# Copies of the relative bias's lines: one write per query row, or a read back to all partitions and a write from there

## The chip, the cores and the metric

One core of a Trainium2 chip runs one program: two transformer blocks over 256 tokens of width 1024 in float32. The metric is the device time of one execution in microseconds (us). In what follows TensorE is called PE as in the profile, VectorE DVE, ScalarE ACT, GpSimd POOL, and SP is the engine that issues the loads of the weights. POOL issues the few transfers that this change is about.

## What is computed

The first block has two layers, each a mixer and an MLP of 4096 hidden columns with a squared ReLU. The second block has a linear recurrence and a causal attention side by side, and a gated MLP. The attention adds a bias to each score which depends on the head and on the distance between query and key alone. Cut to what matters here (with 256 tokens there is one block of keys, so each query sees all keys up to itself):

```python
def sq_relu_mlp(x, w_up, w_down):
    h = jax.nn.relu(x @ w_up)
    return (h * h) @ w_down
...
table_h = rel_table.astype(f32).T
lo = jnp.einsum('bhqd,bhsd->bhqs', qc, ko).astype(f32) * scale
dist_o = tpos[:, None] - (cur * BLK + jnp.arange(BLK))[None, :]
lo = jnp.where(dist_o >= 0, lo + table_h[:, t5_bucket(dist_o)], -jnp.inf)
...
p = jax.nn.softmax(logits, axis=-1)
```

## The kernel before

**Tiling.** A token tile is 128 tokens (P = 128), there are two (TT). Every product with a weight runs as three float32r passes over a split of both sides into a high and a low part: `wh`, `wl` for weights and `xh`, `xl` (or `yh`, `yl` for an MLP's hidden columns) for activations.

**Weights.** They come in units of 256 rows x 512 columns (512 KB). For each unit SP issues a load into a buffer `raw` (line 231, five buffers), ACT casts it to `wh` (line 241, eight buffers) and DVE subtracts to get `wl` (line 242, eight buffers). A load is issued when the unit five before has been split and its `raw` is free; a cast goes on when PE has used the unit eight before. SP issues the loads in the order in which PE uses the units.

**Order on PE.** A small planner (`Line`) runs tasks that are generators: each yields how long after its last product its next operands are there, and of the tasks that can go on, the one of lowest rank does. What comes out is a fixed order of instructions on every engine; the order on DVE, ACT and POOL is made from it by a list scheduler at build time.

**The first block's MLPs.** Both (`mlp0` and `mlp1`) are the same program over eight blocks of 512 hidden columns: `up(b)` takes four units of `w_up`, and `down(b)` takes four units of `w_down`. In the trace the products of an `up` write `mm` (128x256) and those of a `down` write `acc` (128x512). After each `up` ACT applies the ReLU (line 629) and DVE squares it (line 630, tile `hid`).

**The relative bias.** While `mlp1` runs, a task `bias_line` (rank 2) builds `rline`: 8 partitions, one per head, each with a line of LN = 384 floats, which is the negative bias of each distance. It needs one small product (32 buckets x 256 distances) and a copy to SBUF (line 1134). Then POOL issues two transfers, one for four heads each (line 1137). Their destination is `line_d` in DRAM, of which every head has 128 rows that all hold the same line:

```python
line_d = dram.tile([NH, P, LN], F32, name="line_d")
...
nc.gpsimd.dma_start(line_d[hs], rline[hs, None, :].to_broadcast([4, P, LN]))
```

Each is thus 512 rows of 1,536 bytes (768 KB), all read from four partitions of SBUF.

After `mlp1`, in the second block, the task `rel_bias` reads `line_d` back with POOL into the tiles `rel` (line 1317, two transfers of 512 KB): query q's partition reads its row one element earlier than query q-1's, which gives the matrix of distances. DVE uses `rel` in the attention (line 1397).

Of the kernel before, what the change touches and what calls it, by code (L numbers as in the profile page):

```python
# [8 lines left out]
F32 = mybir.dt.float32  # L9
# [6 lines left out]
P = 128  # L16
# [7 lines left out]
# rows of the table of per-partition vectors  # L24
V_PSCALE, V_MQ, V_MK, V_SQ, V_SK, V_Q2, V_K2, V_HG, V_GAMMA, V_N = 0, 6, 8, 10, 11, 12, 13, 14, 15, 31
# and of the gains that go into the weights
# [3 lines left out]
def t5_starts():  # L30
    """First distance of each T5 bucket, and one past the last."""
    bucket = []
    for n in range(S):
        if n < 16:
            bucket.append(n)
        else:
            bucket.append(min(31, 16 + int(math.log(n / 16) / math.log(128 / 16) * 16)))
    return [bucket.index(b) for b in range(32)] + [1 << 20]
# [3 lines left out]
def kernel(  # L42
# [17 lines left out]
    class Stage:  # L60
        """The tiles of one stage; the next stage's take over their bytes."""
# [14 lines left out]
    class Event:  # L76
        """The time from which something is there, once that is known."""
# [6 lines left out]
    class Line:  # L84
        """Orders the tensor engine's work. A task is a generator that yields how long (us) after its last
        product its next one's operands are there, or events to wait for; of the tasks that can go on, the
        one with the lowest rank does."""
# [40 lines left out]
    class Slots:  # L128
        """Lets n tasks at a time hold the buffers of some work."""
# [50 lines left out]
    # -------------------------------------------------------- first loads  # L180
# [3 lines left out]
    # gains that go into the weights, and other small parameters, by feature  # L184
# [11 lines left out]
    # the activation tables are loaded while the first loads are under way  # L196
# [4 lines left out]
    def bcast(dst, vec, eng):  # L201
        """A vector in DRAM to every partition."""
        return eng.dma_start(
            dst, bass.AP(tensor=vec.tensor, offset=vec.offset, ap=[[0, P]] + [list(e) for e in vec.ap]))

    def gain(i):
        """Eight columns of gains, for the k-tiles."""
        return gcols[:, i:i + KT]

    # ------------------------------------------------------------- weights  # L210
    # All products run in float32r passes over exact splits a = hi + lo of both sides:
    # hi hi + hi lo + lo hi. Chunks of weights are loaded and split in the order of their use.
# [4 lines left out]
    def planned(key, segs, nk=KT, row0=0, g=None):  # L217
        """g: first column in gcols of the gains of the weights' rows."""
# [4 lines left out]
    def load_units(segs, nk, row0, g, apart=0):  # L223
        for k0 in range(0, nk, KU):
# [10 lines left out]
            # the split comes after other work that is ready: weights are loaded well ahead  # L235
# [19 lines left out]
    def W(key, ahead=KT):  # L255
        """The split k-tiles of a chunk; the next ones in the order of use are started."""
# [55 lines left out]
    def lin(acc, xt, w, start=True, stop=True):  # L312
        """acc[token, column] (+)= x w, with x as its transposed (hi, lo) k-tiles."""
# [9 lines left out]
    def lin_T(acc, xt, w, c0):  # L323
        """acc[column c0.., token] = (x w)^T."""
# [10 lines left out]
    # ------------------------------------------------------------ constants  # L335
# [4 lines left out]
    # ------------------------------------------------------------- helpers  # L340

    def power(dst, src):
        """src ** -0.5"""
        G.tensor_tensor(dst, src, mhalf[:, :src.shape[-1]], ALU.pow)  # L344

    def xset(name="x"):
        """hi and lo k-tiles of a transposed activation, [feature, k, token]."""
# [7 lines left out]
    def split_T(src, xs, tt, k0, n, by=None):  # L355
        """Columns of src (up to 4 tiles of 128, token-major) to k-tiles k0.. of xs, times by by feature."""
# [5 lines left out]
    def split(pt, xs, tt, k0, n, by=None):  # L362
        """A bank of n tiles to k-tiles k0.. of xs."""
# [15 lines left out]
    class Norm:  # L379
        """Mean square of the rows of a [P, D] tile, gathered by column halves."""  # L380
# [16 lines left out]
        def into(self, xs, tt, g, done):  # L397
            """Normed by the row and g, split and transposed to token tile tt of xs."""
# [20 lines left out]
    def head_rstd(src, nh, hd, sq, name="hs"):  # L419
        """(mean square + eps) ** -0.5 per head of src [P, nh, hd]; sq is scratch."""  # L420
# [7 lines left out]
    def head_norm(src, nh, hd, y):  # L428
        """src [P, nh, hd] over its root mean square per head (no gain) into y."""
# [7 lines left out]
    def exp_T(blocks):  # L437
        """Up to four [P, 128] blocks transposed, side by side."""
# [14 lines left out]
    def residual(tt, c, acc, last=True, lat=1.5, by=None):  # L453
        """h += acc (times by)."""
# [15 lines left out]
    def residual_r(tt, c, acc, last=True):  # L470
        """The one of the first MLP."""
# [4 lines left out]
    def residual_2(tt, c, acc, last=True):  # L476
        """The one of the second MLP."""
# [4 lines left out]
    def residual_ms(tt, c, acc, last=True):  # L482
        """The one before a squared ReLU; that gets h as it is, and its result the reciprocal mean squares."""
# [7 lines left out]
    def add_norms(*sets):  # L491
        """Tasks that write the normed h into sets, a list of (set, gain); the events of each set by token tile."""
# [11 lines left out]
    def turned(xs, src, tt, g, done):  # L504
        """src times the gains g by feature, if any, split and transposed to token tile tt of xs."""
# [5 lines left out]
    def add_turned(xs, g=None):  # L511
        """Tasks that write h to xs, and their events."""
# [19 lines left out]
    def mixer_out(key, xs, cuts, there):  # L532
        """Tasks of h += x w, the rows of w cut into groups; there[token tile][group] are the groups' events."""
# [13 lines left out]
    # ------------------------------------------------------------- the MLPs  # L547

    def mlp(key, xs, there, nb, ku, hidden, finish, ends=1):
        """h += hidden(x up) down in nb blocks of ku * 128 hidden columns; finish(tt, c, acc, last) takes the sums.  # L550
        The last block's part of the last ones can come by itself, in pieces."""
# [13 lines left out]
        def up_one(b, tt):  # L565
            """One token tile: through [token, hidden] and transposes."""
# [78 lines left out]
    # ----------------------------------------------- layer 0: first norms  # L645

    # In the mixers the norms' gains are in the weights, and the root mean squares are put on the products.
# [30 lines left out]
    # the pool mixer's input [feature, k-tile, token], and the queries for the memory  # L678
# [3 lines left out]
    # the pool mixer's windows by feature: k-tile, partitions, group of the window  # L682
# [3 lines left out]
    # window over count for the first tokens  # L686
# [13 lines left out]
    def raw_T():  # L700
        """For a transposed input as it is, in two halves of its k-tiles."""
# [20 lines left out]
    with tc.manual_schedule(engines={ET.DVE, ET.Activation, ET.Pool, ET.PE}):  # L722
        # the first products go on as inputs and weights come in
        x_raw, m_raw = raw_T(), raw_T()
        # products of ones let the tensor engine's clock come up before the weights are there
# [15 lines left out]
        def columns_T(ps, xs, w, k, c0):  # L741
            """More of ps[column, token] from the k-tiles w, which begin at k."""
# [34 lines left out]
        # the rows' root mean squares along the free axis, in every partition  # L777
# [46 lines left out]
    # ----------------------------------------------------- memory attention  # L824
# [3 lines left out]
    def add_mem_kv(l, rank, lat, accs=None):  # L828
        """Keys [feature, head pair, key] and values [key, tile, feature] of layer l, their events and the task;
        accs holds the products if they are under way, lat is the time of the keys' norm."""  # L830
# [13 lines left out]
    def keys_T(acc, r, kT, tt, done, lat):  # L844
        """Four normed heads of 64 in acc's first half to [feature, head pair, key]."""
# [10 lines left out]
    def mem_attention(l, q, xs, tt, q_there, done):  # L856
        """The result for queries q goes to k-tiles 6, 7 of xs."""
# [5 lines left out]
        # the scores get the root mean squares of their queries' heads in the exponential  # L863
# [7 lines left out]
        # the two halves of the array work side by side, into different banks  # L871
# [32 lines left out]
    # -------------------------------------------------- layer 0: pool mixer  # L904
# [669 lines left out]
```

## Time and profile before

| | |
|---|---|
| median of 3 runs | 1080.47 us (1078.93 to 1081.23) |
| the profiled execution, first to last instruction | 1079.3 us |
| PE busy | 1054.1 us (98%) |
| DVE, ACT, POOL busy | 643.0, 562.7, 122.8 us |
| HBM read, written | 181.00 MB, 2.62 MB |
| transfers issued by SP | 180.43 MB |
| transfers issued by POOL | 3.23 MB |

The profile gives the span from the first to the last instruction of one execution, and no other time of that execution. The span lies 1.2 us under the median of the runs and inside their range, so a sum made against the span is carried to the median by adding that difference. A queue's share in the table of DMA queues is the time that its packets took, over 16 DMA engines times the stretch: a share of 50% can be eight engines that are always at work or sixteen that are half the time.

### The profile page before, as it was taken

What the parts mean: (1) busy time and instruction counts of PE and PEld (TensorE: products, weight loads), DVE (VectorE), ACT (ScalarE), POOL (GpSimd) and SP (SyncE); (2) the same over time, 40 slices, a digit from 0 to 9 for tenths busy, and PEclk for the clock granted to TensorE, in tenths of its full rate; (3) what the DMA queues carried; (4) which work ended last, traced back from release to release, by engine and by line L of the source; (5) the groups of instructions that cost most, each with busy time, mean ns of one, the idle gap of its engine ahead of it and who ended that gap; (6) DMA issues with size and microseconds to landing.
All of it is one profiled execution on the core that took longest, in us unless ns stands there. A gap on an engine that the chain in (4) does not pass through costs nothing.

```text
span 1079.3 us, 18396 instructions
## 1 busy us (share of the span) xinstructions
PE 1054.1 (98%) x7352; PEld 927.5 (86%) x7352; DVE 643.0 (60%) x987; ACT 562.7 (52%) x901; POOL 122.8 (11%) x154
## 2 busy tenths in 40 slices
PE   8999999999999996999999998999999999999998
PEld 8768899988876785888988996888999988999997
DVE  5886654554687750755557559766645576454452
ACT  6766544544688640645456443757744466344341
POOL 0524000000152000000001007740000000000000
PEclk9999999999999998899999999999999999999999
DMA  9754465465461456765647552543455556564741
GB/s 317 255 174 157 159 201 187 157 195 195 156 195 41 134 139 116 235 202 177 209 137 232 199 193 81 158 136 113 143 192 182 174 177 213 157 209 150 225 139 40
DMA packets 108551, 184.84 MB, mean 171 GB/s; under 512 B 7769, under 2 KB 32601, under 8 KB 108465
## 3 DMA queue, kind: packets, MB, share of 16 engines
q1 hardware_dynamic: 106560, 180.43, 51.8%
q0 software_dynamic: 1904, 3.23, 2.0%
q8 instruction: 57, 0.93, 0.4%
q14 instruction: 30, 0.24, 0.1%
HBM read 181.00 MB, written 2.62 MB: 170 GB/s over the span
## 4 chain that ended last, share of the span: by engine, by line
PE 91%; DMA 4%; POOL 2%; issue 1%; DVE 1%; ACT 0%; SPq 0%; POOLq 0%; ACTq 0%
PE acc L152 56%; PE mm L152 32%; DMA raw<-in_w_down_dram 3%; PE mm L159 3%; POOL fK L1263 1%; DMA raw<-in_w_in_dram 1%; POOL win L916 0%; DVE wl L242 0%; POOL hs L344 0%; ACT wh L241 0%; POOL hn L431 0%; POOL st L415 0%; POOL win L915 0%; DVE wl L247 0%; POOL st L344 0%
## 5 line engine op out<-in xcount | busy, mean ns | idle before, releaser
L242 DVE TENSOR_TENSOR wl<-raw,wh 128x1024 fp32r<-128x1024 f32 (+1 forms) x315 | 380.6, 1231 | 207.5 <-ACT wh L241 205.1
L241 ACT CAST wh<-raw 128x1024 fp32r<-128x1024 f32 (+1 forms) x315 | 322.0, 1046 | 207.9 <-PE acc L152 108.0
L152 PE MATMUL mm<-xh,wh 128*128 128x256 f32 x752 | 212.9, 283 | 0.0
L152 PE MATMUL mm<-xh,wl 128*128 128x256 f32 x752 | 212.7, 283 | 0.0
L152 PE MATMUL mm<-xl,wh 128*128 128x256 f32 x752 | 212.7, 283 | 0.0
L152 PE MATMUL acc<-wh,yh 128*128 128x512 f32 x342 | 137.2, 401 | 10.2 <-ACT wh L241 10.2
L152 PEld LDWEIGHTS mm<-xh,wh 128*128 128x128 f32 x752 | 144.1, 192 | 1.4 <-issue 0.4
L152 PEld LDWEIGHTS mm<-xl,wh 128*128 128x128 f32 x752 | 144.1, 192 | 1.0
L152 PEld LDWEIGHTS mm<-xh,wl 128*128 128x128 f32 x752 | 144.1, 192 | 0.0
L152 PE MATMUL acc<-wh,xh 128*128 128x512 f32 x336 | 138.7, 413 | 1.3 <-ACT wh L246 1.3
L152 PE MATMUL acc<-wl,yh 128*128 128x512 f32 x342 | 136.4, 399 | 0.9 <-DVE wl L242 0.9
L152 PE MATMUL acc<-wh,yl 128*128 128x512 f32 x342 | 136.0, 398 | 0.0
L152 PE MATMUL acc<-wl,xh 128*128 128x512 f32 x336 | 133.3, 397 | 0.9 <-DVE wl L247 0.9
L152 PE MATMUL acc<-wh,xl 128*128 128x512 f32 x336 | 133.1, 396 | 0.0
L152 PE MATMUL acc<-xh,wh 128*128 128x256 f32 x416 | 118.5, 285 | 1.4 <-ACT wh L241 1.4
L152 PE MATMUL acc<-xh,wl 128*128 128x256 f32 x416 | 118.0, 284 | 1.2 <-DVE wl L242 1.2
L152 PE MATMUL acc<-xl,wh 128*128 128x256 f32 x416 | 117.7, 283 | 0.0
L152 PEld LDWEIGHTS acc<-wh,yh 128*128 128x128 f32 x342 | 65.0, 190 | 25.5 <-ACT wh L241 11.3
L152 PEld LDWEIGHTS acc<-xh,wh 128*128 128x128 f32 x416 | 79.8, 192 | 2.0 <-ACT wh L241 2.0
L152 PEld LDWEIGHTS acc<-xh,wl 128*128 128x128 f32 x416 | 79.8, 192 | 1.8 <-DVE wl L242 1.8
L152 PEld LDWEIGHTS acc<-xl,wh 128*128 128x128 f32 x416 | 79.8, 192 | 0.0
L152 PEld LDWEIGHTS acc<-wl,yh 128*128 128x128 f32 x342 | 65.0, 190 | 15.9 <-DVE wl L242 1.9
(238 smaller groups left out, 1304.5 us busy)
## 6 DMA issues: line engine op xcount, KB each, us to landing
raw<-in_w_in_dram SPq DMA_DIRECT2D x87, 512.0 KB, 4.8
raw<-in_w_up_dram SPq DMA_DIRECT2D x64, 512.0 KB, 4.7
raw<-in_w_down_dram SPq DMA_DIRECT2D x64, 512.0 KB, 4.8
raw<-in_w_out_dram SPq DMA_DIRECT2D x24, 512.0 KB, 4.6
raw<-in_w_ffn_gate_dram SPq DMA_DIRECT2D x44, 256.0 KB, 4.3
raw<-in_w_ffn_up_dram SPq DMA_DIRECT2D x44, 256.0 KB, 4.6
raw<-in_w_ffn_down_dram SPq DMA_DIRECT2D x22, 512.0 KB, 5.2
raw<-in_w_mem_kv_dram SPq DMA_DIRECT2D x8, 512.0 KB, 9.8
```

The source lines that it names most:

```text
L152: PE.matmul(out_, lhsT, rhs, start=start, stop=stop)
L159: PE.transpose(out_, in_, ident)
L241: A.copy(wh[:, ks, :], raw[:, ks, :])
L242: V.tensor_sub(wl[:, ks, :], raw[:, ks, :], wh[:, ks, :].bitcast(F32))
L1263: G.tensor_tensor(k0, k0, f1.to_broadcast([P, 8 * nb, m]), ALU.mult)
```

## The change

`bias_line` no longer writes the 128 copies from `rline`. It writes the eight lines once to a small DRAM tile `lines_d` (12 KB), reads them from there to all 128 partitions of a new SBUF tile `lines` (two transfers of 768 KB, four heads each; every partition reads the same 6 KB), and writes `lines` to `line_d` (two transfers of 768 KB). `line_d` now has the query first and the head second, so that a partition's four heads lie side by side (6,144 bytes), and the read into `rel` has other strides over the same 1,024-byte pieces. The 20 us that the task yields stand ahead of each half instead of behind it. Comments and blank lines apart, this is all:

```diff
-    line_d = dram.tile([NH, P, LN], F32, name="line_d")
+    lines_d = dram.tile([NH, LN], F32, name="lines_d")
+    line_d = dram.tile([P, NH, LN], F32, name="line_d")
     la = line_d[:, :, :]
...
         V.tensor_copy(rline[:, :S], ps[:NH, :S])
+        nc.gpsimd.dma_start(lines_d, rline)
+        lines = act.tile([P, NH, LN], F32, tag="lines", name="lines")
+        l1 = lines_d[:, :]
         for c in range(2):
+            yield 20.0
             hs = slice(4 * c, 4 * c + 4)
-            nc.gpsimd.dma_start(line_d[hs], rline[hs, None, :].to_broadcast([4, P, LN]))
-            yield 20.0
+            nc.gpsimd.dma_start(lines[:, hs, :], bass.AP(tensor=l1.tensor, offset=l1.offset + 4 * c * LN,
+                                                         ap=[[0, P], [LN, 4], [1, LN]]))
+            nc.gpsimd.dma_start(line_d[:, hs, :], lines[:, hs, :])
...
-            nc.gpsimd.dma_start(rel[c], bass.AP(tensor=la.tensor, offset=la.offset + c * 4 * P * LN + P - 1,
-                                                ap=[[LN - 1, P], [P * LN, 4], [1, S]]))
+            nc.gpsimd.dma_start(rel[c], bass.AP(tensor=la.tensor, offset=la.offset + c * 4 * LN + P - 1,
+                                                ap=[[NH * LN - 1, P], [LN, 4], [1, S]]))
```

On POOL, at the place in `mlp1` where the lines are written; before (`st` is the mean square of the norm at the end of `mlp1`, `rel` the read in the second block; in brackets what an instruction waits for, DMASW3 and the like being transfers that POOL issued):

```order
L1137 DMA line_d<-rline 512x1x384 [waits DVE_49,Pool_49]
L1137 DMA line_d<-rline 512x1x384
L415 TENSOR_SCALAR st<-st 128x1 [waits Activation_49]
L344 TENSOR_TENSOR st<-st,mhalf 128x1 [waits Pool_49]
L415 TENSOR_SCALAR st<-st 128x1 [waits Activation_49]
```

and now, at the same place on POOL:

```order
L1137 DMA lines_d<-rline 8x384 [waits DVE_49,Pool_49]
L1143 DMA lines<-lines_d 128x1536 [waits DMASW3_49,PE_49,Activation_49]
L1143 DMA lines<-lines_d 128x1536
L1145 DMA line_d<-lines 128x1536 [waits DMASW4_49]
L1145 DMA line_d<-lines 128x1536 [waits DMASW5_49]
L415 TENSOR_SCALAR st<-st 128x1 [waits Activation_49]
L344 TENSOR_TENSOR st<-st,mhalf 128x1 [waits Pool_49]
```

Two transfers with one wait have become five in three steps, of which each waits for the landing of the one before it; both reads stand ahead of both writes, and what follows on POOL is as it was.

On DVE the order differs at one place, the end of `mlp1`, where the normed rows `xn` of the first token tile are made (line 406) among the splits of the second block's first weights; before:

```order
L459 SCALAR_TENSOR_TENSOR h<-acc,hms,h 128x512 x2
L242 TENSOR_TENSOR wl<-raw,wh 128x1024 x2
L406 TENSOR_SCALAR xn<-h,st 128x512
L242 TENSOR_TENSOR wl<-raw,wh 128x1024
L406 TENSOR_SCALAR xn<-h,st 128x512
L242 TENSOR_TENSOR wl<-raw,wh 128x1024 x2
```

and now, at the same place on DVE:

```order
L459 SCALAR_TENSOR_TENSOR h<-acc,hms,h 128x512 x2
L406 TENSOR_SCALAR xn<-h,st 128x512 x2
L242 TENSOR_TENSOR wl<-raw,wh 128x1024 x5
L373 SCALAR_TENSOR_TENSOR xl<-mm,gcols,xh 128x128 x4
L459 SCALAR_TENSOR_TENSOR h<-acc,hms,h 128x512
```

The two `xn` have moved ahead of three of the five splits. The orders of PE, ACT and SP are the same in both programs.

## Rows read from the trace of the kernel before

**Rows 1.** The page: span, busy time, and the group of casts (busy, mean ns | idle before).

```profile
span 1079.3 us, 18396 instructions
PE 1054.1 (98%) x7352; PEld 927.5 (86%) x7352; DVE 643.0 (60%) x987; ACT 562.7 (52%) x901; POOL 122.8 (11%) x154
...
L241 ACT CAST wh<-raw 128x1024 fp32r<-128x1024 f32 (+1 forms) x315 | 322.0, 1046 | 207.9 <-PE acc L152 108.0
```

**Rows 2.** Waits of PE from 345 to 575 us: total us, times, longest.

```profile
PE acc L152 <- ACT wh L241: 10.2, 2, 5.7
```

**Rows 3.** Stretches: us, busy PE, PEld, DVE, ACT, POOL (instructions); PEclk, DMA share, GB/s.

```profile
106.00:263.00 157.00, 157.00 (x1007) 142.75 (x1006) 86.42 (x90) 74.58 (x88) 0.00 (x0) 1.00 0.56 180
...
419.20:437.60 18.40, 7.29 (x16) 4.50 (x16) 4.78 (x5) 4.78 (x6) 0.00 (x0) 0.63 0.57 138
```

**Rows 4.** PE in order of time: start us, us, line, operation; idle before it, releaser.

```profile
418.72 0.39 PE L152 MATMUL acc<-wl,yh 128*128 128x512 f32 x1
418.95 0.40 PE L152 MATMUL acc<-wh,yl 128*128 128x512 f32 x1
425.09 0.80 PE L152 MATMUL acc<-wh,yh 128*128 128x512 f32 x1 [5.74 <-ACT wh L241]
...
433.29 0.80 PE L152 MATMUL acc<-wh,yh 128*128 128x512 f32 x1 [4.44 <-ACT wh L241]
...
437.60 0.39 PE L152 MATMUL acc<-wh,yl 128*128 128x512 f32 x1
```

**Rows 5.** The chain of waits from 340 to 460 us: start us, us, what.

```profile
396.53 35.56 DMA raw<-in_w_down_dram
```

**Rows 6.** SP's timeline at 395 us; loads issued from 385, 395, 396 us: us to landing.

```profile
395.40 0.37 SPq L231 DMA_DIRECT2D raw<-in_w_down_dram  x1
...
raw<-in_w_down_dram SPq DMA_DIRECT2D x1, 512.0 KB, 4.5
...
raw<-in_w_down_dram SPq DMA_DIRECT2D x1, 512.0 KB, 28.5
...
raw<-in_w_down_dram SPq DMA_DIRECT2D x1, 512.0 KB, 35.6
```

**Rows 7.** The lines' transfers: POOL's timeline, min/median/max us to landing, queue's share 392 to 430.4.

```profile
392.18 2.21 POOL L1137 DMA_DIRECT2D line_d<-rline  x2 [50.01 <-DVE rline L1134]
...
DMA to landing us min/median/max: 35.0/36.5/38.1
...
q0 software_dynamic: 1400, 1.58, 42.2%
```

**Rows 8.** DMA queues and issues from 573 to 580 us: packets, MB, share; us to landing.

```profile
q0 software_dynamic: 282, 1.04, 47.5%
...
raw<-in_w_in_dram SPq DMA_DIRECT2D x3, 512.0 KB, 6.3
rel<-line_d POOLq DMA_DIRECT2D x2, 512.0 KB, 6.1
```

**Rows 9.** DVE's timeline, line 630: fourth and last in mlp0, then in mlp1.

```profile
126.58 0.68 DVE L630 TENSOR_TENSOR hid<-hid 128x512 f32<-128x512 f32 x1
...
262.54 0.68 DVE L630 TENSOR_TENSOR hid<-hid 128x512 f32<-128x512 f32 x1
...
397.56 0.69 DVE L630 TENSOR_TENSOR hid<-hid 128x512 f32<-128x512 f32 x1
...
548.85 0.68 DVE L630 TENSOR_TENSOR hid<-hid 128x512 f32<-128x512 f32 x1
```

**Rows 10.** POOL and DVE at the end of mlp1, in order of time.

```profile
559.78 0.58 POOL L344 TENSOR_TENSOR st<-st,mhalf 128x1 f32<-128x1 f32 x1
...
560.31 1.23 DVE L242 TENSOR_TENSOR wl<-raw,wh 128x1024 fp32r<-128x1024 f32 x1 [1.77 <-ACT wh L241]
...
562.86 0.48 DVE L406 TENSOR_SCALAR xn<-h,st 128x512 f32<-128x512 f32 x1
```

**Rows 11.** The smallest broadcast in the program: its DMA issue, us to landing.

```profile
nsink<-in_sinks_dram POOLq DMA_DIRECT2D x1, 6.0 KB, 2.9
```

## The prediction

> **What bounds the kernel now.** I read the page first. PE is busy for 1054.1 of 1079.3 us [rows 1], so what counts is where PE stands still or runs slowly, and only there can a change of transfers be worth anything. Next I asked for the waits of PE while `mlp1` runs, since the lines of the bias are written there: nearly all of what is listed is 10.2 us in two waits of an `acc` product for a cast on ACT [rows 2]. The same query over `mlp0`, the same program without the bias, lists no wait, and its stretch of 157 us is all busy PE [rows 3]. PE in order of time shows the place: the products of a `down` go every 0.23 us (418.72 to 418.95), then the next one starts at 425.09, six are done, the next starts at 433.29, and the steady pace is back with the one at 437.60 [rows 4]. [...]
>
> The chain of waits says what PE waited for: 35.56 us on a load of `w_down` that was issued at 396.53 [rows 5]. A load of the same size that was issued at 385 landed after 4.5 us; those issued at 395.40 and 396.53 took 28.5 and 35.6 us [rows 6]. What is new between them is POOL's pair of transfers to `line_d`, issued from 392.18 on, which took 35.0 and 38.1 us to land [rows 7].
>
> Why two transfers of 768 KB hold up the others shows in the queue's share. From 392 to 430.4 us POOL's queue had 42.2% of 16 engines for 1.58 MB [rows 7]: 0.422 x 38.4 x 16 = 259 engine-us, which over 36.5 us are 7.1 engines always at work, at 164 engine-us per MB. POOL's own read of `rel`, whose destination is 128 partitions, had 47.5% of 7 us for 1.04 MB [rows 8], 53 engine-us, or 51 per MB, and each of its halves landed in about 6.1 us. [...]
>
> **What the stall costs, in two ways.** Directly: from the product at 418.95 to the one at 437.60 are 18.65 us [rows 4]. Six products between the waits and eight after them make 15 steps, which at 0.23 us are 3.5 us. The loss is 15.2 us, idle time and slow clock together. By comparison: from the fourth square of `hid` to the last are 262.54 - 126.58 = 135.96 us in `mlp0` and 548.85 - 397.56 = 151.29 us in `mlp1` [rows 9]. The difference is 15.3 us, so nothing of the stall is won back later in `mlp1`. I take 15.2.
>
> **The change part by part.**
>
> *Removed:* the two transfers from `rline`, 259 engine-us. With them goes the reason for the late loads, if nothing else holds them up.
>
> *Added, first step:* the write of 12 KB to `lines_d`. On POOL it stands where the old pair stood. The nearest row is the small broadcast of 6 KB, 2.9 us to landing [rows 11]; I take 2.9, so the reads are issued from about 395.1 on. POOL waits for that, for the reads, and for the writes' turn. Behind it on POOL stands only the `st` of the norm, at 559.8 [rows 10], and the whole would have to take 160 us to reach it. So this waiting costs nothing.
>
> *Added, second and third step:* two reads of 768 KB to `lines`, then two writes of 768 KB to `line_d`, 3.15 MB in all where there were 1.57. Their rate is not in the trace. From below I bound it by the `rel` row: 51 engine-us per MB make 160 engine-us, or 10.0 us of all sixteen engines, five for the reads and five for the writes. From above by the old transfer: 164 per MB make 516 engine-us, and if they lay on 7.1 engines, 73 us. I take the first, since the new transfers have 128 partitions on the SBUF side as `rel` has, and the order shows them as 128 rows of 1,536 elements where the old ones were 512 rows from four partitions. [...]
>
> *What hides them.* The load issued at 395.40 has its first product next after 418.95, at about 419.2. Before that come its cast, 1.05 us [rows 1], and its split, 1.23 us [rows 10], so it may land until 416.9: 21.5 us after its issue, of which it needs 4.5. Beside the reads of `rel` the loads landed in 6.3 us [rows 8]. Even if all four new transfers went ahead of it, it would take 4.5 + 10.0 = 14.5 us. So the cover holds by 7 us at the worst of these, and the new transfers cost nothing. If the cover were gone, PE would stand still as it does now, one us for each us of delay and some us of slow clock on top.
>
> *Read of `rel`:* the same 1,024-byte pieces at other strides, 6.1 us to landing, and needed far later, in the attention. Zero.
>
> *The order on DVE at the end of `mlp1`:* the two `xn` now stand ahead of the splits, and they wait for POOL's `st`, which ends at 559.78 + 0.58 = 560.4 [rows 10]. The split that started at 560.31 now comes behind two `xn` of 0.48 us, at about 561.3: 1.0 us later. In return `xn` starts at about 560.4 instead of 562.86. PE has no wait there before, so I take zero, with bounds of 1 us either way.
>
> **The sum.** The span of 1079.3 us goes to 1079.3 - 15.2 = 1064.1. With the 1.2 us by which the median of the runs lies over the span, I predict **1065.3 us**, 1.4% less.
>
> **The rivals.**
>
> *The broadcast read is slow, and the stall comes back longer (slower).* All 128 partitions read the same 6 KB of DRAM, and no row shows such a read of any size. If it went at the pace of the broadcast it replaces, it would take 36.5 us [rows 7], from 395.1 to 431.6, and the writes five more, until 436.6. Now the last of the pair lands at 392.2 + 38.1 = 430.3. The loads would come free 6.3 us later than now, and the loss would be 15.2 + 6.3 = 21.5 us: 1080.5 + 6.3 = **1086.8 us**. It decides from a read of over 30 us, 52 GB/s. For it: it is a broadcast, and the small one needs 2.9 us for 6 KB [rows 11]. [...] Since no row shows a read of this kind, I give the two slow reads 0.16 together.
>
> *The read is half slow.* The load of 395.40 is late when the read ends after 416.9, that is when it takes over 21.8 us (72 GB/s). Between 22 and 30 us the loss lies between nothing and today's 15 us. The middle gives about **1073 us**.
>
> *The change does not do what it says:* the new transfers lie on as few engines as the old ones. The two reads and the two writes then last 36.5 us each, the loads come free at 392.2 + 2.9 + 73 = 468 instead of 430.3, and 38 us are lost on top: **1118 us**. For it: the transfers go through the same queue as before. Against: the 128 rows in the order.
>
> *The loads were not held by the bias's lines*, and the stall stays: **1080 us**. For it: only that the two coincide in time. Against: `mlp0` goes through the same steps with no wait.
>
> **How the numbers follow.** Forecast 0.80; half-slow read 0.10; slow read 0.06; few engines 0.02; stall unchanged 0.02. The forecast's own times go from 1078.9 - 15.3 = 1063.6, the fastest run less the larger loss, down a little for `xn`, to about 1068 (the slowest run less 15.2, the us on DVE and one for loads that come late once). For eight times in ten the range takes in the lower half of the half-slow case: 1063.3 to 1073. Measurements of this kernel can tell about 0.2%, 2.2 us, from no change. Faster: 0.80 + 0.10 = 0.90; within: 0.02; slower: 0.06 + 0.02 = 0.08.
>
> **What would show it.** In the profile of the changed kernel: no wait of an `acc` product for a cast in `mlp1`, the granted clock at 1.00 through it, and 136 us from the fourth square of `hid` to the last. POOL's reads and writes land in 6 to 10 us each and are over by about 415. Loads issued beside them land in 6 to 15 us instead of 28 to 36. If the reads take over 22 us to land, the read was the mistake. If they are fast and PE still waits, then the cover was counted wrongly. If the span falls by less than 15 us though `mlp1` has no stall, look at the end of `mlp1` and the start of the second block.

## The result, and the profile after

The changed kernel takes **1065.86 us** (median of 4 runs, 1064.81 to 1067.20), the one before, measured beside it, 1080.85 us (4 runs, 1078.93 to 1082.42). The ratio is 0.9868 with a 95% interval of 0.9854 to 0.9883: 15.0 us less, where 1065.3 us were predicted, 0.6 us below what was measured.

The page of the changed kernel, with the rows that answer to [rows 1]: span and instructions, busy time of the engines, and the clock granted to PE in 40 slices:

```profile
span 1064.5 us, 18402 instructions
PE 1049.2 (99%) x7352; PEld 924.9 (87%) x7352; DVE 643.3 (60%) x987; ACT 562.6 (53%) x901; POOL 122.7 (12%) x157
PEclk9999999999999999999999999999999999999999
```

The span has fallen from 1079.3 by 14.8 us, and every slice (a 9 stands for 90% or more) is now at 90% or more of the full clock. PE is busy 4.9 us less though it has the same 7352 products: those of the stall ran at a lower clock before, 0.63 on average from 419.2 to 437.6 us [rows 3], at which one took 0.80 us instead of 0.40 [rows 4]. Of the waits from 345 to 575 us, of which [rows 2] shows 10.2 us for a cast, none is left in the list.

The stretches that answer to [rows 3] (us, busy PE, PEld, DVE, ACT, POOL with their instructions, granted clock, share of the DMA engines, GB/s), and the one from 397 to 409 us, in which the new transfers run:

```profile
106.00:263.00 157.00, 157.00 (x1007) 142.70 (x1007) 86.58 (x91) 74.39 (x87) 0.00 (x0) 1.00 0.56 181
397.00:409.00 12.00, 12.00 (x64) 10.18 (x63) 6.50 (x7) 4.08 (x5) 1.07 (x2) 1.00 1.00 364
419.20:437.60 18.40, 18.40 (x116) 16.49 (x116) 9.61 (x10) 6.84 (x8) 0.00 (x0) 1.00 0.69 227
```

Where PE was busy for 7.29 of 18.40 us at a clock of 0.63, it now is for all of them at 1.00. The middle row shows the other side: the DMA engines are all taken for 12 us, and PE doesn't notice.

POOL in order of time (start us, us, line, operation; idle before it and what ended it), where [rows 7] has one pair of transfers:

```profile
391.86 0.53 POOL L1137 DMA_DIRECT2D lines_d<-rline  x1 [49.87 <-DVE rline L1135]
394.15 1.13 POOL L1143 DMA_DIRECT2D lines<-lines_d  x2 [1.77 <-ACT wh L241]
399.03 0.54 POOL L1145 DMA_DIRECT2D line_d<-lines  x1 [3.74 <-DMA lines<-lines_d]
401.99 0.53 POOL L1145 DMA_DIRECT2D line_d<-lines  x1 [2.42 <-DMA lines<-lines_d]
```

And the DMA queues and issues of the same place, 391.5 to 412 us (packets, MB and share of 16 engines; for an issue its size and the median us to landing):

```profile
q0 software_dynamic: 608, 3.16, 42.8%
...
raw<-in_w_down_dram SPq DMA_DIRECT2D x4, 512.0 KB, 8.2
raw<-in_w_up_dram SPq DMA_DIRECT2D x4, 512.0 KB, 8.9
lines<-lines_d POOLq DMA_DIRECT2D x2, 768.0 KB, 5.8
line_d<-lines POOLq DMA_DIRECT2D x2, 768.0 KB, 8.4
```

The two reads landed after 4.6 and 7.0 us (their median stands above as 5.8), the two writes after 7.8 and 9.1, so all was over by about 411. The 1.77 us ahead of the reads end with a cast on ACT, for which they wait too (the order in "The change" has it): the small write had landed at 391.86 + 1.7 = 393.6. POOL's queue took 0.428 x 20.5 x 16 = 140 engine-us for 3.16 MB, 44 per MB, where the old pair took 259 for half of that [rows 7]. The load issued at 395.25, the place at which [rows 6] shows 28.5 and 35.6 us, landed after 7.6 (issues from 394 to 396 us):

```profile
raw<-in_w_down_dram SPq DMA_DIRECT2D x1, 512.0 KB, 7.6
```

DVE in order of time, the rows that answer to [rows 9] for `mlp1` and to [rows 10]:

```profile
397.41 0.68 DVE L630 TENSOR_TENSOR hid<-hid 128x512 f32<-128x512 f32 x1
...
533.57 0.68 DVE L630 TENSOR_TENSOR hid<-hid 128x512 f32<-128x512 f32 x1
...
545.11 0.88 DVE L406 TENSOR_SCALAR xn<-h,st 128x512 f32<-128x512 f32 x2 [1.85 <-POOL st L344]
545.91 5.94 DVE L242 TENSOR_TENSOR wl<-raw,wh 128x1024 fp32r<-128x1024 f32 x5
```

From the fourth square to the last are 136.16 us, what `mlp0` takes, and 15.1 us less than before.

The last square comes 15.28 us earlier, but the end only 14.8. The difference has a row of its own: one wait of PE in the gated MLP, in the list of its waits from 860 us to the end (us in total, times, longest), which the kernel before doesn't have:

```profile
PE mm L159 <- DVE hid L642: 0.5, 1, 0.5
```

It is no larger than the scatter of the runs, and why `hid` comes late there stays open.

### The profile page after: what moved, and what is told of

Same layout as the page of the kernel before. It is cut to its first block, busy times and chain, and to the rows that moved or that the text cites. A ratio compares the mean times of both kernels' runs of the same rounds, so it can differ in the third digit from the quotient of the medians.

```text
span 1064.5 us, 18402 instructions
## 1 busy us (share of the span) xinstructions
PE 1049.2 (99%) x7352; PEld 924.9 (87%) x7352; DVE 643.3 (60%) x987; ACT 562.6 (53%) x901; POOL 122.7 (12%) x157
## 4 chain that ended last, share of the span: by engine, by line
PE 93%; POOL 2%; DVE 1%; DMA 1%; issue 1%; ACT 1%; SPq 0%; ACTq 0%; POOLq 0%
PE acc L152 57%; PE mm L152 33%; PE mm L159 3%; POOL fK L1270 1%; DMA raw<-in_w_in_dram 1%; DMA raw<-in_w_ffn_down_dram 1%; DVE wl L242 1%; POOL win L916 0%; DVE wl L247 0%; ACT wh L241 0%; POOL hs L344 0%; POOL hn L431 0%; POOL st L415 0%; POOL win L915 0%; POOL st L344 0%
## 5 line engine op out<-in xcount | busy, mean ns | idle before, releaser
L152 PEld LDWEIGHTS acc<-wh,yl 128*128 128x128 f32 x342 | 64.3, 188 | 15.4
L152 PEld LDWEIGHTS acc<-wh,xh 128*128 128x128 f32 x336 | 63.4, 189 | 16.1 <-issue 2.5
```

Source lines behind the costliest of these rows:

```text
L152: PE.matmul(out_, lhsT, rhs, start=start, stop=stop)
```

## Experiments

The theory: the pair of transfers that reads four partitions of SBUF side by side holds up the loads of weights beside it, and with them PE. The change does three things at once, though: it takes the source away from these four partitions, lays `line_d` out anew, and takes a detour through DRAM and SBUF. The rivals are that the new layout does it (fewer, longer rows on the DRAM side), that the stall belongs to that place in `mlp1` whatever POOL does there, and, inside the theory, that the few engines (7.1 engines' worth of work [rows 7]) are the cause rather than the place that they read.

All results at once. Each ratio is against the kernel before measured beside it (medians 1080.02 us for e1, e2, e3 and e5, 1079.71 for e4, e6, e7 and e8, 1079.99 for e9 and e10). The fourth column is the time to landing of the two halves of 768 KB that are written to `line_d`, the last the waits of PE for a cast inside `mlp1`, in us. Landings and waits are those of one profiled execution of each kernel.

| kernel | us | ratio, 95% interval | halves | waits |
|---|---|---|---|---|
| e1: old source, new layout | 1079.56 | 0.9994, 0.9985 to 1.0004 | 35.5, 38.2 | 8.9 |
| e2: detour, old layout | 1066.19 | 0.9867, 0.9851 to 0.9883 | 8.4, 9.5 | none |
| e3: DRAM to DRAM, 128 rows | 1065.35 | 0.9857, 0.9842 to 0.9872 | 5.4, 8.3 | none |
| e5: source over 64 partitions | 1066.07 | 0.9866, 0.9848 to 0.9883 | 6.0, 9.3 | none |
| e4: DRAM to DRAM, heads outermost | 1065.98 | 0.9880, 0.9864 to 0.9897 | 14.1, 16.8 | none |
| e8: four partitions, 4 apart | 1065.42 | 0.9872, 0.9857 to 0.9887 | 12.9, 15.6 | none |
| e9: four partitions, 2 apart | 1065.79 | 0.9869, 0.9850 to 0.9888 | 19.5, 22.4 | none |
| e10: four partitions, 32 apart | 1065.75 | 0.9868, 0.9846 to 0.9890 | 22.5, 25.5 | none |
| e6: old pair, 46 us later | 1088.21 | 1.0082, 1.0067 to 1.0098 | 36.9 median | 9.5 |
| e7: old halves 86 us apart | 1088.30 | 1.0086, 1.0071 to 1.0101 | 35.9, 37.5 | 12.2 |

### Which part of the change: layout, detour or source

**The old source with the new layout (e1).** The read of `rel` is that of the changed kernel.

```diff
-    line_d = dram.tile([NH, P, LN], F32, name="line_d")
+    line_d = dram.tile([P, NH, LN], F32, name="line_d")
...
-            nc.gpsimd.dma_start(line_d[hs], rline[hs, None, :].to_broadcast([4, P, LN]))
+            nc.gpsimd.dma_start(bass.AP(tensor=la.tensor, offset=la.offset + 4 * c * LN,
+                                        ap=[[LN, 4], [NH * LN, P], [1, LN]]),
+                                rline[hs, None, :].to_broadcast([4, P, LN]))
...
```

> One part of the change alone: line_d has its new layout (query first, head second) and the read into rel the new strides, but the copies still come straight from the four partitions of rline. If the source on few partitions is what clogs (my theory), both transfers take about 36 us to land as before, PE waits again and the time is that of before, 1080 to 1082 us. If the layout of the destination was what made the old transfers slow (rival), they land in under 15 us and the time is about 1066 us.

It measured 1079.56 us, no different from before (and 0.4 us under what was expected). Waits of PE from 345 to 590 us:

```profile
PE acc L152 <- ACT wh L241: 8.9, 2, 5.4
...
```

And the landing of what is read from `rline` (us, min/median/max):

```profile
DMA to landing us min/median/max: 35.5/36.8/38.2
```

The stall and the slow landing are those of [rows 2] and [rows 7]. The layout alone does nothing.

**The detour with the old layout (e2).** The changed kernel, with `line_d` and the read of `rel` as before; the write puts a partition's four lines at four places.

```diff
...
-            nc.gpsimd.dma_start(line_d[:, hs, :], lines[:, hs, :])
+            nc.gpsimd.dma_start(bass.AP(tensor=la.tensor, offset=la.offset + 4 * c * P * LN,
+                                        ap=[[LN, P], [P * LN, 4], [1, LN]]), lines[:, hs, :])
...
```

> The other part alone: lines go to DRAM, are read back to 128 partitions and written from there as in the changed kernel, but line_d keeps its old layout, so that each partition writes four pieces of 1,536 bytes. My theory: the writes come from 128 partitions, land in under 12 us, no wait of PE in mlp1, 1065 to 1067 us. If the layout is what counts, the writes take some 36 us and the time is 1080 us or more.

1066.19 us and no wait of PE from 345 to 590 us: the whole gain without the layout.

**No detour through SBUF (e3).** The changed kernel without the tile `lines`; the copies go from `lines_d` to `line_d`, DRAM to DRAM.

```diff
-        lines = act.tile([P, NH, LN], F32, tag="lines", name="lines")
...
-            nc.gpsimd.dma_start(lines[:, hs, :], bass.AP(tensor=l1.tensor, offset=l1.offset + 4 * c * LN,
-                                                         ap=[[0, P], [LN, 4], [1, LN]]))
-            nc.gpsimd.dma_start(line_d[:, hs, :], lines[:, hs, :])
+            nc.gpsimd.dma_start(line_d[:, hs, :], bass.AP(tensor=l1.tensor, offset=l1.offset + 4 * c * LN,
+                                                          ap=[[0, P], [LN, 4], [1, LN]]))
```

> The SBUF tile lines left out: lines_d is copied from DRAM to line_d in DRAM, 128 rows of 6,144 bytes in each half, all rows read from the same 6 KB. Half the bytes of the changed kernel and one step less. If rows spread over all engines are enough (my theory), each half lands in 4 to 8 us, no wait of PE, 1065 to 1067 us. If a read of one place by all engines is slow, and was hidden in the changed kernel by the order of its steps, the halves take over 20 us and the time is 1070 us or more.

1065.35 us. The DMA issues from 391 to 404 us:

```profile
line_d<-lines_d POOLq DMA_DIRECT2D x2, 768.0 KB, 6.8
```

The halves landed after 5.4 and 8.3 us, as fast as from SBUF (7.8 and 9.1), with half the bytes moved.

**No detour at all (e5).** The kernel before, with the lines built in 128 partitions instead of 8: the table is repeated 16 times per head ahead of the small product, and each half is read from 64 partitions, of which each serves eight rows. The layout is the old one.

```diff
...
+        wide = act.tile([32, NH, 16], F32, tag="wide", name="wide")
+        G.tensor_copy(wide, table[:, :, None].to_broadcast([32, NH, 16]))
...
-        mm(ps[:NH, :S], table, inb)
+        mm(ps[:, :S], wide.rearrange("p h j -> p (h j)"), inb)
...
-            nc.gpsimd.dma_start(line_d[hs], rline[hs, None, :].to_broadcast([4, P, LN]))
+            hs = slice(64 * c, 64 * c + 64)
+            nc.gpsimd.dma_start(bass.AP(tensor=la.tensor, offset=la.offset + 4 * c * P * LN,
+                                        ap=[[8 * LN, 64], [LN, 8], [1, LN]]),
+                                rline[hs, None, :].to_broadcast([64, 8, LN]))
```

> The old transfers with one thing changed: their source. The small product makes each head's line in 16 partitions (128 in all) instead of one, and each partition writes 8 of the 128 copies; bytes, rows of 1,536 bytes and layout of line_d are as before, there is no read back. My theory (few source partitions) says that each half lands in 5 to 10 us, no wait of PE, 1065 to 1067 us. If rows of 1,536 bytes written to DRAM straight from SBUF are the slow thing, they take 36 us again and the time is 1080 us.

1066.07 us. The DMA issues from 391 to 404 us:

```profile
line_d<-rline POOLq DMA_DIRECT2D x2, 768.0 KB, 7.7
raw<-in_w_down_dram SPq DMA_DIRECT2D x3, 512.0 KB, 9.1
```

So the detour isn't needed either. What e2, e3 and e5 have in common with the changed kernel, and e1 lacks, is the source: no longer four neighbouring partitions. None of them beats the changed kernel: their intervals overlap its own, and with no wait left in `mlp1` there is nothing more to gain there.

### Does the stall follow the transfers

**The pair later (e6).** The kernel before, with the pair issued some 46 us later.

```diff
         G.memset(rline[:, S:], -NEG)
-        yield 20.0
+        yield 65.0
         ps = mm_bank()
```

> The kernel before with the lines made 45 us later by the planner's clock: the task yields 65 us instead of 20 ahead of its small product, all else is as before. If the old transfers cause the stall (my theory), it moves with them: the fourth to the fifth square of hid take the usual 15 us, PE waits 40 to 50 us later than before, and the loss is 13 to 17 us, 1079 to 1082 us. If the stall belonged to its place in mlp1 and the transfers only coincide, it stays at 419 us.

It measured 1088.21 us, outside of what was expected. Waits of PE from 345 to 590 us:

```profile
PE acc L152 <- ACT wh L241: 9.5, 2, 5.9
PE mm L159 <- DVE xn L406: 3.5, 1, 3.5
...
```

PE in order of time, at the new place:

```profile
463.68 0.40 PE L152 MATMUL acc<-wh,yl 128*128 128x512 f32 x1
470.00 0.79 PE L152 MATMUL acc<-wh,yh 128*128 128x512 f32 x1 [5.92 <-ACT wh L241]
...
477.34 0.79 PE L152 MATMUL acc<-wh,yh 128*128 128x512 f32 x1 [3.59 <-ACT wh L241]
```

POOL's timeline has the pair:

```profile
438.11 2.21 POOL L1137 DMA_DIRECT2D line_d<-rline  x2 [96.63 <-DVE rline L1134]
```

It was issued 46 us later than before, and the stall went with it: two waits for a cast again, the same drop to products of 0.79 us, 45 us after [rows 4]. This part came as expected. What was missed is the other wait, 3.5 us at the end of `mlp1`, which has to do with `xn` and not with the transfers. DVE there, in order of time:

```profile
565.31 1.22 DVE L242 TENSOR_TENSOR wl<-raw,wh 128x1024 fp32r<-128x1024 f32 x1 [0.17 <-ACT wh L241]
...
567.11 2.35 DVE L242 TENSOR_TENSOR wl<-raw,wh 128x1024 fp32r<-128x1024 f32 x2
...
570.04 1.22 DVE L242 TENSOR_TENSOR wl<-raw,wh 128x1024 fp32r<-128x1024 f32 x1
571.17 0.88 DVE L406 TENSOR_SCALAR xn<-h,st 128x512 f32<-128x512 f32 x2
```

The scheduler made another order out of the later task and put `xn` behind eight splits instead of two: it starts at 571.17, where the kernel before has it at 562.86 [rows 10]. The spans differ by 1085.3 - 1079.3 = 6.0 us, and the stall is not where they come from: the fourth square to the last are 396.18 to 548.25, a loss of 16.1 against 15.3 us, but the fourth came 1.4 us earlier, so that the last is still 0.6 us ahead of the kernel before. Behind the wait for `xn` PE is late: a product that starts there at 570.11 starts here at 574.90, 4.8 us later. So 5.4 us are lost between, of which the wait is 3.5; the granted clock, 0.89 from 560 to 575 us, is the likely rest. The last 1.2 us are lost after that, 0.6 of them in a wait for `hid` near the end that the kernel before doesn't have. The medians differ by 8.5 us. The execution in the profile is the fastest of the four (1087.03 us, 1.2 under their median), so no row covers the whole of that.

**One half at a time (e7).** The kernel before, with two tiles `rline`; the second half has its product, copy and transfer 86 us after the first.

```diff
...
         for c in range(2):
-            hs = slice(4 * c, 4 * c + 4)
+            hs, rline = slice(4 * c, 4 * c + 4), rlines[c]
+            yield 20.0 if c == 0 else 68.0
+            ps = mm_bank()
+            mm(ps[:NH, :S], table, inb)
+            V.tensor_copy(rline[:, :S], ps[:NH, :S])
             nc.gpsimd.dma_start(line_d[hs], rline[hs, None, :].to_broadcast([4, P, LN]))
-            yield 20.0
```

> The kernel before with its two transfers apart: the line is made twice, and the second half is written some 68 us after the first. If a load is as late as its slowest engine (my theory), one transfer alone clogs its engines as long as the pair did: each lands in 30 to 36 us, PE stands still twice and the time is 1088 to 1096 us. If what counts is how many bytes are in the way at a time, each half delays the loads half as long, the cover hides much of it, and the time is below 1080 us.

1088.30 us, 8.6 us more than before: PE stands still at both halves, and the two stalls cost some 24 us where that of the pair costs 15. Waits of PE from 345 to 575 us:

```profile
PE acc L152 <- ACT wh L241: 7.3, 2, 5.7
PE mm L152 <- ACT wh L241: 4.9, 1, 4.9
...
```

The DMA queues and issues from 391 to 427 us, around the first half alone:

```profile
q0 software_dynamic: 704, 0.79, 22.5%
...
raw<-in_w_down_dram SPq DMA_DIRECT2D x3, 512.0 KB, 30.3
...
line_d<-rline POOLq DMA_DIRECT2D x1, 768.0 KB, 35.9
```

And the issues from 477 to 515 us, around the second:

```profile
raw<-in_w_up_dram SPq DMA_DIRECT2D x4, 512.0 KB, 30.7
line_d<-rline POOLq DMA_DIRECT2D x1, 768.0 KB, 37.5
```

One half takes as long as the two together (35.9 against 36.5 us), at 0.225 x 36 x 16 = 130 engine-us, which over 35.9 us are 3.6 engines. So the halves don't slow each other; each is slow by itself. And 3.6 engines' worth of traffic makes the loads beside it nearly as late (30.3 and 30.7 us) as 7.1 did (28.5 and 35.6 [rows 6]), so the share of sixteen engines that is taken says little about the harm.

The traces also hold each packet by itself, with its size, start and time, and two things can be counted there. First, packets in flight: of the larger packets of POOL's queue, those that carry the lines, the old pair has hardly ever more than 8 in flight at a time, and 8 for over half of its time; one half here has hardly ever more than 4. If an engine has one packet in flight at a time, which is an assumption (the some 16 in flight in e3 and e5 fit it), a share of 22.5% is thus four engines nearly always at work, and not sixteen now and then. Second, the loads' own packets: from 410 to 424 us in the kernel before, with the pair under way, those of 2 KB take 0.09 us each on average, and from 385 to 391 us, ahead of the pair, 0.11 us. The loads are late because packets of theirs start late, not because they are slow once started. That they queue behind the pair's on the same engines would fit this but is not shown: the traces don't say which engine a packet ran on.

### Few engines, or few places that they read

In the old pair both come together: 7.1 engines' worth of work with hardly ever more than 8 packets in flight, and four partitions side by side. The next four kernels keep few engines, as far as packets in flight show that, and change the places: in all of them hardly more than 8 of the lines' packets are in flight at any time.

**DRAM to DRAM with the heads outermost (e4).** As e3, but with the old layout, whose outermost dimension is the four heads.

```diff
...
+            nc.gpsimd.dma_start(line_d[hs], bass.AP(tensor=l1.tensor, offset=l1.offset + 4 * c * LN,
+                                                    ap=[[LN, 4], [0, P], [1, LN]]))
...
```

> Few engines without few partitions: lines_d is copied from DRAM to line_d in DRAM with the four heads as the slowest dimension and the old layout, so that the shape of the old transfers is kept, but nothing is read from SBUF. If the number of engines alone made the old ones slow, the halves land in about 36 us and the time is 1080 us. If the four neighbouring partitions that all of a transfer's engines read from were slow (the packets of the old ones took three times as long per byte as those over 128 partitions), each half lands in 10 to 15 us, on few engines at the usual pace; the load issued at 395 us then lands before 416.9 and the time is 1065 to 1068 us.

1065.98 us. The queues and issues from 391.5 to 420 us:

```profile
q0 software_dynamic: 1440, 1.60, 16.1%
...
line_d<-lines_d POOLq DMA_DIRECT2D x2, 768.0 KB, 15.5
```

And the issues from 394 to 397.9:

```profile
raw<-in_w_down_dram SPq DMA_DIRECT2D x3, 512.0 KB, 11.8
```

0.161 x 28.5 x 16 = 73 engine-us, over the 16.8 us to the later landing some 4 engines' worth of work: few engines, more than twice as long as e3, but 46 engine-us per MB and not 164. The loads are late by some 7 us, which the cover (the 21.5 us that the prediction gives a load before PE needs it) swallows. Few engines by themselves cost little here: the loads landed after 11.8 us, and PE has no wait.

**Four partitions, 4 apart (e8).** The kernel before, with each head's line built in four partitions side by side, of which the transfer reads one: the sources are partitions 0, 4, 8, 12 for the first half and 16, 20, 24, 28 for the second. The rest of the transfer is the same, 512 rows of 1,536 bytes from four partitions.

```diff
...
+        wide = act.tile([32, NH, 4], F32, tag="wide", name="wide")
+        G.tensor_copy(wide, table[:, :, None].to_broadcast([32, NH, 4]))
...
-            nc.gpsimd.dma_start(line_d[hs], rline[hs, None, :].to_broadcast([4, P, LN]))
+            one = rline[16 * c:16 * c + 16:4, None, :]
+            nc.gpsimd.dma_start(line_d[hs], one.to_broadcast([4, P, LN]))
```

> The old transfers from four partitions of SBUF each, but the four do not lie side by side: the small product makes each head's line in four partitions (32 in all), and one of each four is the source, so that they are four apart. Bytes, rows and layout as before. [...] If that is what made the old transfers slow, the halves now land in 10 to 15 us and the time is 1065 to 1068 us. If four partitions are slow wherever they lie, or four engines are, they take 36 us and the time is 1080 us.

1065.42 us. The queues and issues from 391.5 to 420 us:

```profile
q0 software_dynamic: 1408, 1.59, 18.1%
...
line_d<-rline POOLq DMA_DIRECT2D x2, 768.0 KB, 14.2
```

And the issues from 394 to 398:

```profile
raw<-in_w_down_dram SPq DMA_DIRECT2D x3, 512.0 KB, 11.3
```

0.181 x 28.5 x 16 = 83 engine-us, 52 per MB, the price of `rel` [rows 8]. The number of partitions, of rows and the bytes are those of the old pair, and the stall is gone. What is dear here is that the four partitions are neighbours: 164 engine-us per MB and 36.5 us to landing, against 52 and 14.2.

**Two apart (e9) and 32 apart (e10).** The same with other distances. First partitions 0, 2, 4, 6, with each line built in two partitions:

```diff
...
+            one = rline[8 * c:8 * c + 8:2, None, :]
+            nc.gpsimd.dma_start(line_d[hs], one.to_broadcast([4, P, LN]))
```

Then partitions 0, 32, 64, 96 (the second half 16, 48, 80, 112), with each line in 16:

```diff
...
+            one = rline[16 * c:P:32, None, :]
+            nc.gpsimd.dma_start(line_d[hs], one.to_broadcast([4, P, LN]))
```

> As the kernel with the source partitions four apart, but two apart (0, 2, 4, 6 and 8, 10, 12, 14). If four neighbouring partitions share one way to the DMA engines that carries about 768 KB in 34 us (from the old pair's landing), two of each four sources share one here, so a half needs about 17 us and lands in 17 to 20 us, between 14 us (four apart) and 36 us (side by side). The loads beside it land before 416.9 us, so no wait of PE, 1064 to 1068 us. If any distance over one is enough, it lands in 14 us.

> The source partitions are 32 apart (0, 32, 64, 96, and 16, 48, 80, 112). [...] If only neighbours share, or none do, it lands in about 14 us as with four apart. Either way no wait of PE, 1064 to 1068 us.

They took 1065.79 and 1065.75 us. Two apart, the queues and issues from 391.5 to 420 us:

```profile
q0 software_dynamic: 1408, 1.59, 28.7%
...
line_d<-rline POOLq DMA_DIRECT2D x2, 768.0 KB, 21.0
```

And the issues from 394 to 400:

```profile
raw<-in_w_down_dram SPq DMA_DIRECT2D x3, 512.0 KB, 17.8
```

32 apart, the queues and issues from 391.5 to 420 us:

```profile
q0 software_dynamic: 1408, 1.59, 30.3%
...
line_d<-rline POOLq DMA_DIRECT2D x2, 768.0 KB, 24.0
```

And the issues from 394 to 400:

```profile
raw<-in_w_down_dram SPq DMA_DIRECT2D x3, 512.0 KB, 17.6
```

Both land late: two apart after 19.5 and 22.4 us, where 17 to 20 were expected, and 32 apart after 22.5 and 25.5, where it would have been about 14 if only neighbours share or none do.

In order the halves land after 36.5 us (neighbours), 24.0 (32 apart), 21.0 (two apart) and 14.2 (four apart), and the engine-us per MB are 164, 87, 82 and 52. The packets show the same one by one: three rows of 1,536 bytes (4,608) take 0.74 us on average from neighbours, 0.38 and 0.36 from 32 and two apart, 0.21 from four apart, and 0.18 from DRAM (e4). If partitions were slow simply by standing close, 32 apart would be the best of all; it is nearer to two apart than to four apart (24.0 us against 21.0 and 14.2). A packet from neighbours takes about twice as long as one from two or 32 apart, and these 1.7 to 1.8 times as long as one from four apart. That neighbours share one way to the DMA engines is the supposition of e9's expectation; the 21.0 us of two apart, between 36.5 and 14.2, come near its 17 to 20, but no run shows such a way, and it gives no reason for the 24.0 us of 32 apart. What the runs show is the order of the four distances, and not its cause. Why 32 apart is 3 us slower than two apart stays open too.

These two also test the cover that the prediction counted, 21.5 us from issue to landing: loads of 17.6 and 17.8 us cause no wait, loads of 30.3 (e7) do.

## Why the prediction was right, point by point

- **What bounds the kernel, and the price of the stall.** It came to 15.2 and 15.3 us by two ways. The medians differ by 15.0 us, the spans by 14.8, and the fourth square to the last by 15.1. The step that read the loss from PE's own rows, slow clock included (0.63 on average from 419.2 to 437.6 us [rows 3]), carried the forecast; the list of waits alone (10.2 us) would have given a third too little.
- **Why the loads were late.** The blame on the pair is shown: it moves the stall (e6), one half alone makes one (e7), and other ways to write the same bytes don't (e2, e3, e5, e4, e8, e9, e10). The reason given was only half right. The prediction put the price of 164 engine-us per MB down to few engines and four partitions without parting them. Few engines' worth of work is there: 3.6 and some four packets in flight for one half in e7. But e4 and e8 have few too (73 and 83 engine-us, hardly more than 8 packets in flight) and no stall. What makes the old pair dear is that its four source partitions are neighbours (164 engine-us per MB, 52 with four apart in e8); the same source on sixteen engines was not run. The forecast came out all the same because the change removes both at once, few engines and neighbouring sources; it was luck that it didn't have to know which of them counts.
- **First step, 2.9 us for the small write.** It landed after 1.7 us, and POOL issued the reads at 394.15 instead of 395.1, though a cast on ACT held them for about half a us, a wait that the sum didn't have. POOL's wait cost nothing, as said.
- **Second and third step, 160 engine-us, 6 to 10 us each, over by 415.** 140 engine-us; 4.6 and 7.0 us for the reads, 7.8 and 9.1 for the writes, over by 411. The bound by `rel` was the right end to take. That the work would spread over all sixteen engines was the author's estimate, by the likeness to `rel` and the 128 rows, and no run shows that rows of this kind bring it about; what the trace shows of the new transfers is up to some 16 packets in flight at a time.
- **The cover.** The load of 395.25 landed at 402.9, 14 us ahead of the 416.9 that it had; the worst case had left 7. Loads beside the transfers took up to 12.8 us, inside the 6 to 15.
- **The order on DVE, zero with 1 us either way.** `xn` waited 1.85 us for POOL's `st` with splits behind it, and PE has no wait there. e6 shows what the zero hid: in the other direction, behind more splits, the same instruction makes PE wait for 3.5 us. The term was right for this order only.
- **The rivals.** The broadcast read isn't slow: 128 partitions read the same 6 KB of DRAM in 4.6 and 7.0 us for 768 KB, two under way at once, where 22 us were needed to do harm. That removes the slow and the half-slow read. Few engines for the new transfers: 44 engine-us per MB, 4.6 to 9.1 us to landing and up to some 16 packets in flight say no. A stall that stays: gone.
- **The last 0.5 us** (span down by 14.8 instead of 15.3) are the one wait for `hid` near the end, not the end of `mlp1` or the start of the second block, where the prediction said to look: product by product PE's lead over the kernel before is 15.3 to 15.5 us from the stall up to that wait, and 14.8 behind it.

## What to carry to other kernels

A transfer off the critical path can set its pace by making the loads beside it late (28.5 and 35.6 us here, 4.5 ahead of the pair [rows 6]), so look for what was issued just before the first late load, and price it in engine-us per MB against another transfer of the same profile: three times the price (164 against 51) was the sign here. When copies of a few lines are to be written, look at which partitions they are read from; spreading the source (6.0 and 9.3 us in e5, 12.9 and 15.6 in e8), or moving it to DRAM (5.4 and 8.3 us in e3), was enough here, where neighbours took 35.0 and 38.1, and the detour through `lines` wasn't needed. Price the stall from the engine's own rows, with the products that run at the lower clock behind each wait (0.80 us each instead of 0.40 [rows 4]).

## What was not expected of the hardware

Four neighbouring partitions as the source of a broadcast gave 768 KB in 36.5 us, about 21.5 GB/s, and four that lie four apart gave it in 14.2 us. Partitions 32 apart, which I would have taken for the most independent, were slower than four apart: 24.0 us. One such transfer on 3.6 engines' worth of traffic delays 512 KB loads nearly as much (30.3 us) as two on 7.1 (28.5 and 35.6 us). A broadcast from a single 6 KB place of DRAM had no price that shows, to SBUF (4.6 and 7.0 us) or to DRAM (5.4 and 8.3 us).
